# Loading W_v head by head, filler matmuls, an evenly spread conv finish and GLU blocks through a contiguous tile, in a hybrid conformer and attention block

## The chip, the cores and the metric

The kernel runs on the 8 cores of one Trainium2 chip, one batch element on each core (2048 positions of 2048 channels). The metric is the device time of the slowest core, in microseconds (us). Executions come in two states. In the slow one the cores of a die are recorded at a lower TensorE clock and the time is some per cent longer.

PE is TensorE, ACT is ScalarE, DVE is VectorE, POOL is GpSimd and SP is SyncE.

## The reference, cut to what matters

```python
h = rms_norm(x, ln1_g)
u = einsum("bsd,de->bse", h, w_in)                  # 2048 -> 5 x 1024
c_val, c_gate, q, k, v = split(u)
# conv_mixer(c_val, c_gate, ...)
g = c_val * sigmoid(c_gate)                         # GLU
y = causal_depthwise_conv(g, w_dw, width=31) + b_dw
y_conv = silu(layer_norm(y, over channels))
# attention in chunks of 64, each over itself and 8 chunks before, with a bias by distance
y_attn = chunked_relbias_attention(q, k, v, ...)
y = concat([rms_norm(y_conv), rms_norm(y_attn)])    # 1024 + 1024 channels
x = x + einsum("bse,ed->bsd", y, w_out)
x = x + relu(rms_norm(x) @ w_ff1)**2 @ w_ff2        # 2048 -> 8192 -> 2048
```

## The kernel before

The program is first recorded as a list of operations. A greedy list scheduler, which works with modelled durations, then puts them into one fixed order for each engine. The scheduler's rule is short (its latencies and its DMA rate are not measured here):

```python
# every engine: take, of the operations modelled as ready, the one that comes first in the program
o.prio = o.i + self.off
...
for s in succ[i]:                       # when a consumer becomes ready, in the model
    lat = XLAT                          # 180 ns from engine to engine
    if so.eng == "pe" and e != "pe":
        lat += SLACK                    # 400 ns more before PE may count on a result
    rt[s] = max(rt[s], o.end + lat)
...                                     # a DMA: bytes / DMA_BPNS (310) after the DMA before it, + 2000 ns
```

Stage 1 normalizes 16 tiles of x (128 rows each), transposes them on PE into `hT`, and multiplies them with W_v, which comes in four quarters of 256 columns:

```python
for j in range(4):
    ld.append(P.dma("pool", f"wv{j}", wv[:, j, :, :], wv_d[j]))
    ...                                          # x tiles 1 to 4 after quarter 0
for t in range(NT):
    norm_tile(xs1[t % 5], t, ...)                # squares on ACT, scaling on DVE, 16 PE transposes
    ...
    for hf in range(4):
        for k in range(16):
            mm(ps(hf, 0, 256), hT[:, qd, k, ti*128:(ti+1)*128], wv[:, hf, k, :], k == 0, k == 15)
        act(V[:, t, 2*hf:2*hf+2, 0:128], ..., AF.Identity)
```

Stage 2 is the q and k projection with the attention. Stage 3 is the conv: for each of 8 channel blocks (`cc`) and 4 row quarters (`qd`) two gate products, the GLU, and a depthwise product with Toeplitz matrices (`pad`). The GLU result `G` is transposed in 32x32 blocks by DVE straight into the scattered layout of `Gt`:

```python
stt(G[:, :], th[:, :], 1.0, ps(1), ALU.add, ALU.mult)
o_ = bass.AP(gt, 1 + 16 * qd, [[32 * 66, 128], [1, 16], [66, 32]])     # 66 elements from one to the next
P.vtr(o_, G[:, :].rearrange("p (b i) -> p b i", i=32), slow=3.6)
```

Stage 4 finishes the conv (LayerNorm, SiLU, sums of squares) while the output projection already runs. For a row quarter, `fin_cc` does this eight times:

```python
def fin_cc(qd, cc):
    stt(yy, yy, pc(bdw2 + cc), ysum[qd], ALU.add, ALU.subtract)   # DVE
    tt(yy, yy, rs[:, :], ALU.mult)                                 # DVE
    act(z, yy, AF.Silu, ...)                                       # ACT; in the trace y<-y,pv
    P.ts(yb[:, s, qd, 0, :], z, pc(goc + cc), ALU.mult)            # DVE
    act(jk, z, AF.Square)                                          # ACT; in the trace yb<-y, for quarter 0
    for j in range(4):
        mm(..., jk[j], onesb[:, 0:1], ...)                         # PE, 1 column: onesb,yb

def out_tr(t):                                                     # attention half of tile t
    for k in range(8): P.tr(...)                                   # PE: identb,on
    act(yT[:, :, :], ..., AF.Identity)                             # ACT: yT<-ps

def out_attn(t):
    ... mm(ps(b), yT[:, k, :], wo[:, 0, cb, k, :], ...)            # PE: wo,yT, 32 of 512 columns
...
for c in range(8):
    fin_cc(0, c)
fin_end(0)
...
out_tr(0)
out_attn(0)
```

After the last gate product, PE has only the depthwise rest, the small sums `onesb,yb` and the projection `wo,yT` to do. That hand-over from the gates to the projection is called **the switch** below. Stage 5 is the feed-forward part (FFN).

## Time and profile before

2785.49 us median (four fast runs, 2784.37 to 2788.06). From the profiled run's milestones, the mean of the 8 cores:

| part of the kernel | us |
|---|---|
| start to last W_v matmul | 181.6 |
| attention, to its last matmul before the gates | 320.8 |
| gates, to the last gate matmul | 226.0 |
| switch, from the last gate matmul to the last depthwise matmul | 34.7 |
| output projection, to the last `wo,yb` | 241.3 |
| FFN, from its first `hTb,yb` to the end | 1773.8 |
| end, with 1.9 between the last `wo,yb` and the FFN | 2780.1 |

A milestone is the start of the last matmul with the named operands, if not said otherwise.

The engine table and the shares of the chain of waits, on the profile page of the kernel before (busy us, share of the span, instructions; then the share of each engine in the chain that ended last):

```profile
PE 2707.2 (97%) x14445; PEld 1327.1 (48%) x14704; DVE 932.3 (34%) x1482; ACT 830.9 (30%) x1601; POOL 228.1 (8%) x365
...
PE 94%; DMA 2%; issue 2%; DVE 1%; ACT 1%; ACTq 0%; DVEq 0%; SPq 0%; POOLq 0%
```

PE is busy 97% of the time, and the chain is 94% PE. What can be won is PE's idle and half-clock time. By the view of stretches most of it lies at the start and, in smaller part, behind the switch (start:end, length, busy us and instructions of PE, of its weight loads, of DVE, ACT and POOL, then granted clock, DMA share, GB/s), kernel before, core 0:

```profile
20.00:60.00 40.00, 18.55 (x149) 14.06 (x147) 17.29 (x17) 19.30 (x31) 1.26 (x3) 0.74 1.00 261
700.00:900.00 200.00, 185.16 (x1246) 91.70 (x1268) 157.31 (x216) 121.36 (x167) 34.01 (x33) 0.97 0.55 144
```

From 20 to 60 us PE works less than half of the time, at a mean clock of 0.74, while the DMA engines are full (1.00). The waits of PE in the whole run say what it waits for (total us, times, longest), kernel before:

```profile
PE ps L163 <- DVE hb_78 L198: 10.7, 6, 4.4
PE ps L163 <- DVE hb_77 L198: 10.3, 5, 3.2
PE ps L163 <- DVE hb_79 L198: 7.1, 1, 7.1
```

`hb` is a normalized x tile. PE waits for tiles that arrive one by one, beside whole quarters of W_v: from issue to landing an x tile took 15.1 to 26.8 us (medians by buffer, core 0, 0 to 80 us) and a quarter 15.0 us. The groups of instructions show the cost of the scattered transpose (busy us and mean ns after the bar, idle time before), kernel before:

```profile
L206 DVE STREAM_TRANSPOSE Gt_112<-G 128x512 bf16<-128x512 bf16 x16 | 39.3, 2458 | 1.5
```

### The profile page before, as it was taken

What the parts mean: (1) busy time and instruction counts of PE and PEld (TensorE: products, weight loads), DVE (VectorE), ACT (ScalarE), POOL (GpSimd) and SP (SyncE); (2) the same over time, 40 slices, a digit from 0 to 9 for tenths busy, and PEclk for the clock granted to TensorE, in tenths of its full rate; (3) what the DMA queues carried; (4) which work ended last, traced back from release to release, by engine and by line L of the source; (5) the groups of instructions that cost most, each with busy time, mean ns of one, the idle gap of its engine ahead of it and who ended that gap; (6) DMA issues with size and microseconds to landing.
All of it is one profiled execution on the core that took longest, in us unless ns stands there. A gap on an engine that the chain in (4) does not pass through costs nothing.

```text
span 2782.1 us, 38484 instructions; the slowest of 8 cores (2778.2 to 2782.1 us)
## 1 busy us (share of the span) xinstructions
PE 2707.2 (97%) x14445; PEld 1327.1 (48%) x14704; DVE 932.3 (34%) x1482; ACT 830.9 (30%) x1601; POOL 228.1 (8%) x365
## 2 busy tenths in 40 slices
PE   4999999999989999999999999999999999999999
PEld 3875555444444544444444444444444444444444
DVE  3236665655787522022131130220311302202113
ACT  4428887311376431211202102112022021120120
POOL 0000000422500000000000000000000000000000
PEclk8999999999999999999999999999999999999999
DMA  9411110324655478454444444579544444444424
GB/s 243 103 31 36 34 28 11 61 46 76 122 152 167 152 155 177 77 76 76 76 76 76 76 76 76 76 151 196 123 76 76 76 76 76 76 78 76 77 43 137
DMA packets 112455, 256.86 MB, mean 92 GB/s; under 512 B 5393, under 2 KB 83217, under 8 KB 94609
## 3 DMA queue, kind: packets, MB, share of 16 engines
q0 software_dynamic: 92112, 167.82, 37.9%
q1 hardware_dynamic: 20162, 86.56, 9.3%
q8 instruction: 122, 2.00, 0.3%
q14 instruction: 59, 0.48, 0.1%
HBM read 388.60 MB, written 33.55 MB: 152 GB/s over the span
## 4 chain that ended last, share of the span: by engine, by line
PE 94%; DMA 2%; issue 2%; DVE 1%; ACT 1%; ACTq 0%; DVEq 0%; SPq 0%; POOLq 0%
PE ps L159 93%; DMA xa_71<-x 1%; PE ps L163 1%; DMA acc<-out 1%; DMA wc_105<-wcg 0%; DVE y L198 0%; DVE y L192 0%; DVE hb_77 L198 0%; DVE Gt_113 L206 0%; ACT L178 0%; ACT hb_77 L178 0%; DVE hb_78 L198 0%; DVE y L206 0%; DVE yb L203 0%; DVE h2b L198 0%
## 5 line engine op out<-in xcount | busy, mean ns | idle before, releaser
L192 DVE TENSOR_TENSOR acc<-acc,ps 128x512 f32<-128x512 f32 x512 | 351.8, 688 | 1413.3 <-PE ps L159 1401.9
L159 PE MATMUL ps<-yb,fT 128*128 128x512 bf16 x2699 | 596.4, 379 | 4.0 <-DVE acc L192 1.1
L159 PEld LDWEIGHTS ps<-yb,fT 128*128 128x128 bf16 x2752 | 269.1, 98 | 326.3 <-issue 2.1
L178 ACT ACTIVATE rl_134<-ps 128x512 f32<-128x512 f32 x128 | 76.4, 597 | 1102.5 <-PE ps L159 1101.0
L159 PE MATMUL ps<-w2s_138,fT 128*128 128x512 bf16 x1317 | 292.4, 379 | 1.4
L159 PE MATMUL ps<-hTb,yb 128*128 128x512 bf16 x1024 | 242.2, 379 | 0.0
L159 PE MATMUL ps<-yb 128*128 128x512 bf16 x992 | 237.6, 379 | 1.7
L159 PEld LDWEIGHTS ps<-w2s_138,fT 128*128 128x128 bf16 x1344 | 131.5, 98 | 158.6
L225 POOL DMA_DIRECT2D yb<-w x75 | 66.6, 888 | 1173.8 <-PE ps L159 1105.6
L159 PEld LDWEIGHTS ps<-yb 128*128 128x128 bf16 x1024 | 100.2, 98 | 120.8
L159 PEld LDWEIGHTS ps<-hTb,yb 128*128 128x128 bf16 x1024 | 100.2, 98 | 120.3
L178 ACT ACTIVATE rl_135<-ps 128x512 f32<-128x512 f32 x128 | 76.4, 597 | 271.1 <-PE ps L159 271.1
L159 PE MATMUL ps<-wv,hT 128*128 128x256 bf16 x1024 | 120.6, 281 | 5.4 <-DMA wv<-wv 4.0
L159 PE MATMUL ps<-hTb,w1s_136 128*128 128x512 bf16 x512 | 121.0, 379 | 0.0
L159 PE MATMUL ps<-hTb,w1s_137 128*128 128x512 bf16 x512 | 121.0, 379 | 0.0
L159 PE MATMUL ps<-wo,yT 128*128 128x512 bf16 x497 | 117.1, 383 | 3.9 <-ACT yT L178 2.2
L159 PE MATMUL ps<-yb,w1s_136 128*128 128x512 bf16 x480 | 119.3, 379 | 1.7
L159 PE MATMUL ps<-yb,w1s_137 128*128 128x512 bf16 x496 | 117.5, 379 | 0.8
L159 PE MATMUL ps<-hT,wc_105 128*128 128x512 bf16 x498 | 115.0, 381 | 3.4 <-DMA wc_105<-wcg 2.5
L159 PE MATMUL ps<-hT,wc_104 128*128 128x512 bf16 x496 | 117.4, 379 | 0.9
L159 PE MATMUL ps<-wo,yb 128*128 128x512 bf16 x496 | 113.4, 379 | 0.8
L159 PEld LDWEIGHTS ps<-wv,hT 128*128 128x128 bf16 x1024 | 102.6, 101 | 20.6 <-issue 6.3
(300 smaller groups left out, 2741.1 us busy)
## 6 DMA issues: line engine op xcount, KB each, us to landing
yb<-w POOLq DMA_DIRECT2D x75, 1024.0 KB, 10.2
w2s_138<-w POOLq DMA_DIRECT2D x21, 1024.0 KB, 9.5
w1s_136<-w POOLq DMA_DIRECT2D x16, 1024.0 KB, 9.3
w1s_137<-w POOLq DMA_DIRECT2D x16, 1024.0 KB, 9.4
acc<-out SPq DMA_DIRECT2D x16, 1024.0 KB, 11.8
out<-acc SPq DMA_DIRECT2D x64, 256.0 KB, 7.5
wo<-wo POOLq DMA_DIRECT2D x8, 1024.0 KB, 13.4
xs_127<-x SPq DMA_DIRECT2D x6, 1024.0 KB, 6.4
```

Of the source, the lines that this page charges most:

```text
L159: self.op("pe", lambda e: e.matmul(out, lhsT=lhsT, rhs=rhs, start=start, stop=stop, skip_group_check=skip), [lhsT, rhs], [out], f * max(n ...
L163: self.op("pe", lambda e: e.transpose(out, in_, ident), [in_, ident], [out], 64.0)
L178: self.op("act", lambda e: e.activation(out=out, in_=in_, func=func, scale=scale, bias=bias, **kw), r, w, d).func = func
L192: self._ew(eng, lambda e: e.tensor_tensor(out=out, in0=in0, in1=in1, op=op), [in0, in1], [out], fast)
L225: o = self.op(eng, lambda e: e.dma_start(out=out, in_=in_), r, w, 900.0 if eng == "pool" else 350.0, dma=True, key=key, nbytes=nb)
```

## The change

The intent: (1) load x tiles and single heads of W_v in turn, two loads in flight, so that PE has work early; (2) fill PE's early gaps with matmuls of ones, meant to keep its clock from being halved (before, core 0's was recorded at 0.50 from 36.7 to 53.8 us); (3) transpose the GLU blocks into a contiguous tile, and let ACT do the reordering copy; (4) spread the conv finish evenly over the output tiles, and let the scheduler count on results for PE 300 ns later (SLACK). The core of the diff:

```diff
-SLACK = 400.0
+SLACK = 700.0
-DMA_BPNS = 310.0
+DMA_BPNS = 320.0
...
+    def fill_gaps(self, until, reach):     # after scheduling: matmuls of ones where the model sees PE idle
...
         self.schedule()
+        self.fill_gaps(60000.0, 0.8)
...
+LAZY = 0.0                                 # optional extra slack for some matmuls, unused at 0
...
-    wv_d = dr("wv", [4, 128, 16, 256])
+    wv_d = dr("wv", [8, 128, 16, 128])
...
+    chain = [o_gr, xo_[0]]
+    for it in ("w0", "x1", "w1", "x2", "w2", "x3", "w3", "x4", "w4", "x5", "w5", "x6", "w6", "x7", "w7"):
...
+        chain.append(o_)
...
-        for hf in range(4):
-            for k in range(16):
-                mm(ps(hf, 0, 256), hT[:, qd, k, ti * 128:(ti + 1) * 128], wv[:, hf, k, :], k == 0, k == 15)
-            act(V[:, t, 2 * hf:2 * hf + 2, 0:128], ..., AF.Identity)
+        for e0, n in VG[min(t, 8)]:        # heads that are there already, in groups of 4, 2 or 1
+            vgroup(t, e0, n)
+        if t < 8:
+            for tt_ in range(t + 1):       # the new head for all tiles so far
+                vgroup(tt_, t, 1)
+    for k in range(2, len(chain)):
+        chain[k].deps.add(chain[k - 2].i)  # two loads in flight
...
+    Gc = sb("Gc", [512], BF16, D0 + 34 * KB)      # shares its place with th and yT
...
-        o_ = bass.AP(gt, 1 + 16 * qd, [[32 * 66, 128], [1, 16], [66, 32]])
-        P.vtr(o_, G[:, :].rearrange("p (b i) -> p b i", i=32), slow=3.6)
+        P.vtr(Gc[:, :], G[:, :])
+        act(gt[:, :, 1 + 16 * qd:17 + 16 * qd], bass.AP(Gc, 0, [[512, 128], [1, 32], [32, 16]]), AF.Identity)
...
-    seq = [("c", 0), ("f", 1, 0, 4), ("a", 2), ("c", 1), ("f", 1, 4, 8), ("c", 2), ("s", 2), ("a", 3), ("c", 3), ("f", 2, 0, 3), ...
+    seq = [("c", 0), ("f", 1, 0, 2), ("a", 2), ("c", 1), ("f", 1, 2, 5), ("c", 2), ("f", 1, 5, 8), ("a", 3), ("c", 3), ("s", 2), ...
```

In `seq`, "a" and "c" are the two halves of an output tile, "s" the statistics and "f" pieces of the finish of a row quarter.

More of the change, by code (lines that the diff above doesn't have):

```diff
@@ L22 @@
 XLAT = 180.0
-SLACK = 400.0
+SLACK = 700.0
 TABLE = 1300.0
 DMA_LAT = 2000.0
-DMA_BPNS = 310.0
+DMA_BPNS = 320.0
 SEM_EPOCH = 30000
+FILL = 216.0
 class Op:
-    __slots__ = ("i", "func", "eng", "fn", "dur", "deps", "dma", "key", "cnt", "bytes", "prio",
+    __slots__ = ("i", "func", "lazy", "eng", "fn", "dur", "deps", "dma", "key", "cnt", "bytes", "prio",
                  "start", "end", "pos", "signal", "waits", "ins")
@@ L47, in __init__ @@
         self.func = None
+        self.lazy = 0.0
 class Prog:
@@ L154, in n, with mm @@
         return k
-    def mm(self, out, lhsT, rhs, start, stop, skip=False):
+    def mm(self, out, lhsT, rhs, start, stop, skip=False, lazy=0.0):
         n = self.n(rhs)
@@ L159, in mm, with filler @@
         self.op("pe", lambda e: e.matmul(out, lhsT=lhsT, rhs=rhs, start=start, stop=stop, skip_group_check=skip),
-                [lhsT, rhs], [out], f * max(n / 2.37, 64.0))
+                [lhsT, rhs], [out], f * max(n / 2.37, 64.0)).lazy = lazy
+    def filler(self, out, lhsT, rhs):
+        self.fill = (lambda e: e.matmul(out, lhsT=lhsT, rhs=rhs, start=True, stop=True, skip_group_check=True),
+                     [self.last_w[k] for k in self.keys(lhsT)][0])
+    def fill_gaps(self, until, reach):
+        fn, dep = self.fill
+        order, t = [], 700.0
+        for o in self.order["pe"]:
+            k = max(0, int((o.start - t - SLACK - XLAT) * reach / FILL)) if o.start < until else 0
+            for _ in range(k):
+                f = Op(len(self.ops), "pe", fn, FILL)
+                f.deps.add(dep)
+                f.start = f.end = o.start
+                self.ops.append(f)
+                order.append(f)
+                self.seq.insert(self.seq.index(o), f)
+            order.append(o)
+            t = max(t, o.end)
+        for j, o in enumerate(order):
+            o.pos = j
+        self.order["pe"] = order
     def tr(self, out, in_, ident):
@@ L296, in schedule @@
                 if so.eng == "pe" and e != "pe":
-                    lat += SLACK
+                    lat += SLACK + so.lazy
                 rt[s] = max(rt[s], o.end + lat)
@@ L482, in build_program @@
     wqk = [sb(f"wqk{i}", [16, 128], BF16, o + 16384 + 4096 * i) for i in range(3)]
-    wv = sb("wv", [4, 16, 256], BF16, C)
+    wv = sb("wv", [8, 16, 128], BF16, C)
     on = sb("on", [16, 1024], BF16, C)
@@ L493, in loadx @@
         xo_[t] = P.dma("sp", f"xa{t % 5}", xs1[t % 5][:, :], x_d[t * 128:(t + 1) * 128, :])
+        return xo_[t]
     def bcast(g, n):
         return bass.AP(gv_d.tensor, g * 2048, [[0, 128], [1, n]])
+    P.memset(onesb[:, :], 1.0, "dve")
+    P.memset(onef[:, :], 1.0, "dve")
+    P.filler(ps(3), onesb[:, :], bass.AP(onesb, 0, [[128, 128], [0, 4], [1, 128]]))
     gr = sb("gr", [2048], F32, D0 + 42 * KB)
-    P.dma("sp", "gr", gr[0:1, :], gv_d[0:1, :])
+    o_gr = P.dma("sp", "gr", gr[0:1, :], gv_d[0:1, :])
     loadx(0)
@@ L502, in build_program @@
     P.dma("sp", "pv", pv[:, :], pv_d)
-    P.memset(onef[:, :], 1.0, "dve")
     for j in range(4):
@@ L509, in build_program @@
             act(g1[:, j * 512:(j + 1) * 512], ps(4 + j), AF.Identity)
-    ld = []
-    for j in range(4):
-        ld.append(P.dma("pool", f"wv{j}", wv[:, j, :, :], wv_d[j]))
-        if j == 0:
-            for t in range(1, 5):
-                loadx(t)
-            P.dma("sp", "sel", sel[:, :], id_d[:, 0:4])
+    chain = [o_gr, xo_[0]]
+    for it in ("w0", "x1", "w1", "x2", "w2", "x3", "w3", "x4", "w4", "x5", "w5", "x6", "w6", "x7", "w7"):
+        j = int(it[1])
+        if it[0] == "w":
+            o_ = P.dma("pool", f"wv{j}", wv[:, j, :, :], wv_d[j])
+        elif j < 5:
+            o_ = loadx(j)
+        else:
+            o_ = ("x", j)
+        chain.append(o_)
+    P.dma("sp", "sel", sel[:, :], id_d[:, 0:4], after=chain[4].i)
     P.ts(pv[:, bdw2:bdw2 + 8], pv[:, bdw:bdw + 8], 2.0, ALU.mult)
@@ L519, in build_program @@
     tt(pc(gqk), pc(52), pc(53), ALU.mult)
-    P.memset(onesb[:, :], 1.0, "dve")
     P.memset(oh[:, :], 0.0, "dve")
@@ L539, in norm_tile, with vgroup @@
             dst(hf, psh[:, b * 1024:(b + 1) * 1024].rearrange("p (k c) -> p k c", c=128))
+    VG = []
+    for t in range(9):
+        e, gs = 0, []
+        while e < t:
+            n = next(n for n in (4, 2, 1) if e % n == 0 and e + n <= t)
+            gs.append((e, n))
+            e += n
+        VG.append(gs)
+    nvb = [0]
+    def vgroup(t, e0, n):
+        qd, ti = divmod(t, 4)
+        b = nvb[0] % 3
+        nvb[0] += 1
+        for k in range(16):
+            rhs = wv[:, e0:e0 + n, k, :] if n > 1 else wv[:, e0, k, :]
+            mm(ps(b, 0, 128 * n), hT[:, qd, k, ti * 128:(ti + 1) * 128], rhs, k == 0, k == 15)
+        act(V[:, t, e0:e0 + n, 0:128], ps(b, 0, 128 * n).rearrange("p (h c) -> p h c", c=128), AF.Identity)
     for t in range(NT):
@@ L555, in build_program @@
             mark = len(P.ops) - 1
-        for hf in range(4):
-            for k in range(16):
-                mm(ps(hf, 0, 256), hT[:, qd, k, ti * 128:(ti + 1) * 128], wv[:, hf, k, :], k == 0, k == 15)
-            act(V[:, t, 2 * hf:2 * hf + 2, 0:128], ps(hf, 0, 256).rearrange("p (h c) -> p h c", c=128), AF.Identity)
-    for j in (1, 2, 3):
-        ld[j].deps.add(xo_[2 * j - 1].i)
+        for e0, n in VG[min(t, 8)]:
[3 more added lines that the diff above has]
+                vgroup(tt_, t, 1)
+    chain = [xo_[c[1]] if isinstance(c, tuple) else c for c in chain]
+    for k in range(2, len(chain)):
+        chain[k].deps.add(chain[k - 2].i)
+    for t in range(8, NT):
+        xo_[t].deps.add(chain[-2].i)
     q32 = [sb(f"q32{i}", [512], F32, D0 + 40 * KB + 2048 * i) for i in range(2)]
@@ L592, in proj @@
                     for j in range(4):
-                        mm(ps(2, j, j + 1), sq[b][:, j * 128:(j + 1) * 128], onesb[:, 0:1], True, True)
+                        mm(ps(2, j, j + 1), sq[b][:, j * 128:(j + 1) * 128], onesb[:, 0:1], True, True, lazy=LAZY)
                     act(kst[:, qd, :], ps(2, 0, 4), AF.Ln, scale=1.0 / 128, bias=pc(epsc))
@@ L717, in conv_dw @@
             act(cs[:, :], yy, AF.Square, scale=0.5, bias=pc(bdw + cc))
-            mm(ps(7)[0:4, :], oh[:, 3 - qd:7 - qd], cs[:, :], cc == 0 and qd == 0, cc == 7, skip=True)
+            mm(ps(7)[0:4, :], oh[:, 3 - qd:7 - qd], cs[:, :], cc == 0 and qd == 0, cc == 7, skip=True, lazy=LAZY)
             su = ysum[qd][:, :]
@@ L760, in fin_cc @@
         for j in range(4):
-            mm(ps(FB, j, j + 1), bass.AP(jk.tensor, jk.offset + j * 128, [list(jk.ap[0]), [1, 128]]), onesb[:, 0:1], cc == 0 and j == 0, cc == 7, skip=True)
+            mm(ps(FB, j, j + 1), bass.AP(jk.tensor, jk.offset + j * 128, [list(jk.ap[0]), [1, 128]]), onesb[:, 0:1], cc == 0 and j == 0, cc == 7, skip=True, lazy=LAZY)
     def fin_end(qd):
@@ L859, in build_program @@
     fin_stats(1)
-    seq = [("c", 0), ("f", 1, 0, 4), ("a", 2), ("c", 1), ("f", 1, 4, 8), ("c", 2), ("s", 2), ("a", 3), ("c", 3), ("f", 2, 0, 3),
-           ("a", 4), ("c", 4), ("f", 2, 3, 6), ("a", 5), ("c", 5), ("f", 2, 6, 8), ("a", 6), ("c", 6), ("s", 3), ("a", 7), ("c", 7),
-           ("f", 3, 0, 3), ("a", 8), ("c", 8), ("f", 3, 3, 6), ("a", 9), ("c", 9), ("f", 3, 6, 8)]
-    for t in range(10, NT):
+    seq = [("c", 0), ("f", 1, 0, 2), ("a", 2), ("c", 1), ("f", 1, 2, 5), ("c", 2), ("f", 1, 5, 8), ("a", 3), ("c", 3), ("s", 2),
+           ("a", 4), ("c", 4), ("f", 2, 0, 2), ("a", 5), ("c", 5), ("f", 2, 2, 5), ("a", 6), ("c", 6), ("f", 2, 5, 8), ("a", 7), ("c", 7), ("s", 3),
+           ("a", 8), ("c", 8), ("f", 3, 0, 3), ("a", 9), ("c", 9), ("f", 3, 3, 6), ("a", 10), ("c", 10), ("f", 3, 6, 8), ("a", 11), ("c", 11)]
+    for t in range(12, NT):
         seq += [("a", t), ("c", t)]
@@ L984, in _prep_shared @@
     wvv = win[:, 4096:5120]
-    wv = np.stack([kc(wvv[:, i * 256:(i + 1) * 256], 256) for i in range(4)])
+    wv = np.stack([kc(wvv[:, i * 128:(i + 1) * 128], 128) for i in range(8)])
     wcg = np.stack([np.stack([kc(win[:, o + i * 128:o + (i + 1) * 128], 128) for o in (0, 1024)], 1) for i in range(8)])
```

## The prediction

> **What bounds the kernel now.** TensorE: the engine table gives PE 2707 of 2782 us busy (97%), the chain of waits is 94% PE. Only time in which PE is idle or half-clocked can be won. By the table of stretches it is lost in two places.
>
> (a) Start, 0 to 75.5 us. PE is dense only from 75.5 us (timeline). By then it has done 8 tiles' transposes (128 at 56 ns) and 114 of the 1024 W_v matmuls (256 columns, 109 ns apart when dense): about 20 us of useful work. The DMA share is about 1.0 from 2 to 67 us: 12 x tiles and the 4 W_v quarters move in 65 us. [...] With whole quarters PE has little to do per loaded byte; the waits list charges 28 us to hb (tiles arriving late). Short bursts also leave the granted clock at 0.50 from 37 to 53 us and near 62 and 72 us. [...]
>
> (b) Conv finish, 700 to 900 us: PE idle 12.4 + 2.4 us, three half-clock steps nearby; waits on ACT yb, jk, yT, cs, rct; DVE is 83 to 100% busy at 730-750 us. 500-700 us loses about 5 more. The FFN (PE over 99%) doesn't change.
>
> **What the change does.**
> 1. x0,w0,...x7,w7, at most two in flight. After pair t, 2t+1 units (tile x head, 16 x 56 ns = 0.9 us) become ready, against about 6.6-7 us per pair of loads: PE becomes dense near tile 3 to 4, at 38-45 us, with 18-20 us of work done. The last pair lands at 55-62 us. 640 narrow matmuls at 56 ns, 64 at 109, 320 at 215 come to the same 112 us, so narrow groups cost nothing. W_v now ends at 182 us; I expect 147 to 160: gain 28 us (22 to 36), all on the critical path. The static order assumes DMA times; where they are late PE stalls, so I don't book the full 36.
> 2. Some 35 fillers of 0.22 us (0.43 cold), nearly all before tile 0 is transposed. They cost at most 1-2 us and keep the clock up: 2-4 us, counted in 1.
> 3. GLU blocks: 32 DVE transposes of 2.46 us with scattered output become contiguous ones (estimate 0.4-0.75 us, from 0.73 us for the f32 transpose of y) plus an ACT copy (estimate 0.6-0.75 us, from 0.62 us for jk). DVE sheds about 55 us, ACT gains about 20; off the path except near 730-750 us.
> 4. Even finish and larger slack: the stalls at 730-750 and 790-805 us shrink. 3 and 4 together: 9 us (2 to 16) of about 24.
>
> **Predicted: 2785.6 - 28 - 9 = 2749 us**, 80% range 2736 to 2764. Faster by over 2% (under 2730): 0.05; within 2%: 0.94; slower: 0.01.
>
> **What would show it.** W_v's last matmul at 147-160 us; PE dense from 40-45 us, no long 0.50 clock after 15 us; DVE transposes of G under 0.8 us; PE idle at 700-900 us halved; the FFN's length unchanged to 2 us.
>
> **What would make it wrong.** Gaps between loads with two in flight: DMA share well below 1 before 60 us, PE dense only after 55 us, gain 15 us. The new order or ACT's extra copies stalling PE in the conv stage (step 4 gives nothing). Conversely, if start and finish both reach their floor, 2730.

The "6.6-7 us per pair of loads" are the author's estimate; at the 259 GB/s recorded from 2 to 67 us a pair (1536 KB) would take 6.1 us. What the trace of before shows are half-clock records that last 3.41 us or a multiple of it, but for each core's last one: on core 0 17.07 us of them from 36.7 us on, with PE busy for 5.26 us from 37 to 53 us. That fillers would keep the clock up, and for 2 to 4 us, was the author's estimate.

## The result, and the profile after

The changed kernel has fast runs of 2768.62 and 2766.56 us. Two more were slow (2981.03 and 2956.98) and are not used. The ratio is 0.9934, with a 95% interval of 0.9911 to 0.9958: 0.66% faster, in the class "within 2%". A ratio here is the mean time of one kernel's fast runs over that of the other's fast runs of the same rounds, so it is not quite the ratio of the quoted medians. The predicted 2749 us, range 2736 to 2764, is missed: the two runs lie 2.6 and 4.6 us above the range, and about half of the gain came.

Milestones, the mean of 8 cores of the profiled runs (both fast):

| part | before | after | change | predicted |
|---|---|---|---|---|
| start to last W_v matmul | 181.6 | 161.1 | -20.5 | -28 |
| attention | 320.8 | 318.5 | -2.3 | 0 |
| gates | 226.0 | 227.1 | +1.1 | -9 for gates, switch and output together |
| switch | 34.7 | 41.7 | +7.0 | |
| output projection | 241.3 | 237.1 | -4.2 | |
| FFN | 1773.8 | 1774.2 | +0.4 | 0 |
| end | 2780.1 | 2761.6 | -18.5 | -37 |

So two things are to be explained: 7.5 us that are missing at the start, and a conv stage that lost 3.9 us where 9 were to be won. The switch is the worst line of the table.

The page of the kernel after, in the same two views as shown of before:

```profile
PE 2729.5 (99%) x14737; PEld 1299.8 (47%) x14737; DVE 880.7 (32%) x1482; ACT 871.2 (31%) x1641; POOL 229.0 (8%) x369
...
PE 94%; DMA 4%; ACT 1%; issue 1%; DVE 1%; SPq 0%; ACTq 0%; DVEq 0%; POOLq 0%
```

PE's 99% looks better than it is: half-clocked matmuls and fillers count as busy too (the first 27 fillers for 10.4 us, on core 0 at 427 ns each until 17.2 us and not 216). DMA has doubled its share of the chain. The stretches of the kernel after, core 0, with the two worst of 10 us added:

```profile
20.00:60.00 40.00, 33.78 (x423) 28.09 (x424) 18.59 (x19) 22.45 (x47) 2.64 (x5) 0.91 0.92 210
700.00:900.00 200.00, 183.48 (x1171) 89.85 (x1171) 148.38 (x210) 136.96 (x179) 16.92 (x16) 0.92 0.49 140
710.00:720.00 10.00, 2.15 (x52) 1.82 (x52) 9.91 (x14) 8.65 (x15) 5.72 (x6) 0.51 1.00 204
720.00:730.00 10.00, 8.01 (x36) 3.40 (x37) 5.43 (x7) 5.10 (x9) 1.71 (x2) 0.64 0.35 67
```

PE's idle time at 700 to 900 us was 14.8 us and is 16.5 us now, where I predicted half. From 710 to 720 us PE is busy for only 2.15 us, and the clock stays near half afterwards (its records on core 0 say half from 710.2 us on, for 17.1 us). The start has improved a lot, but the DMA share fell from 1.00 to 0.92. The groups of the GLU transpose after:

```profile
L231 DVE STREAM_TRANSPOSE Gc<-G 128x512 bf16<-128x512 bf16 x32 | 22.7, 710 | 2.9
L203 ACT ACTIVATE Gt_113<-Gc 128x512 bf16<-128x512 bf16 x16 | 17.1, 1072 | 43.0 <-DVE Gc L231 42.9
```

The transpose fell from 2458 to 710 ns, as predicted. The ACT copy takes 1072 ns, where I had estimated 600 to 750. Its output lies in runs of 16 elements but its input is read with a stride of 32. A contiguous ACT operation of that size from f32 (`yb<-y`) takes 614 ns here; no run tests the stride alone. In the whole program DVE lost 51.6 us of work and ACT gained 40.3, twice the 20 predicted; 34.2 of these are the copies. In the scattered output of the old DVE transpose neighbours lay 66 elements apart; the traces show that it is slower (2458 ns against 710), not why.

### Where the start loses

The chain of waits of the kernel after begins like this (start, length, what):

```profile
1.48 5.01 DMA xa_71<-x
6.56 8.51 DMA xa_72<-x
15.14 6.87 DMA xa_73<-x
...
69.64 3.73 PE ps L161 x64
```

Each x tile is issued only when the x tile before it has landed (each load waits for the one two before it in an alternating list). On core 0 a pair of loads takes 7.43 us: the heads of W_v were issued at 12.64 and, six pairs later, at 57.22 us. Core 0 has the slowest pairs; the mean of the 8 cores is 7.20 us. I had predicted 6.6 to 7 us for a pair, and PE dense from 38 to 45 us. PE is dense only from 69.6 us. The last head of W_v had landed at 64.8 us, so the loads alone don't explain this. The timeline of ACT, core 0, shows what stood in between:

```profile
67.33 1.91 ACT L203 ACTIVATE hb_79<-xa_74 128x2048 bf16<-128x2048 f32 x1 [2.18 <-DMA xa_74<-x]
69.23 0.59 ACT L203 ACTIVATE V<-ps 128x128 bf16<-128x128 f32 x3
```

ACT idles for 2.18 us until the ninth x tile lands, and the copy of `V` that PE needs stands behind the work on this tile. So PE's waits up to 165 us name a second suspect, ACT (kernel after, core 0; the mean of the cores is 9.7 us for both lines together):

```profile
PE ps L161 <- ACT V L203: 4.2, 2, 2.3
PE ps L161 <- ACT hT L203: 2.6, 2, 2.2
```

### Where the switch loses

PE's timeline after the last gate matmul, kernel after, core 0 (start, length, operands, count, and in brackets the idle time before and what ended it):

```profile
711.84 0.25 PE L161 MATMUL ps<-onesb,yb 128*128 128x1 bf16 x4 [4.06 <-ACT yb L203]
715.14 0.24 PE L161 MATMUL ps<-onesb,yb 128*128 128x1 bf16 x4 [3.06 <-ACT yb L203]
...
722.48 1.44 PE L161 MATMUL ps<-wo,yT 128*128 128x512 bf16 x3 [1.48 <-ACT yT L203]
```

For 15 us PE does little but tiny sums, each waiting for ACT. The projection `wo,yT`, which would fill the time, begins at 722.48 us. It needs `yT`, and the timeline of ACT shows where that copy stands, first before and then after:

```profile
732.53 1.02 ACT L178 ACTIVATE yT<-ps 128x1024 bf16<-128x1024 bf16 x1 [1.09 <-PE ps L159]
...
734.87 0.81 ACT L178 ACTIVATE y<-y,pv 128x512 f32<-128x512 f32 x1
```

```profile
709.38 0.81 ACT L203 ACTIVATE y<-y,pv 128x512 f32<-128x512 f32 x1
710.10 1.08 ACT L203 ACTIVATE Gt_114<-Gc 128x512 bf16<-128x512 bf16 x1
711.08 0.61 ACT L203 ACTIVATE yb<-y 128x512 bf16<-128x512 f32 x1
...
720.51 0.80 ACT L203 ACTIVATE y<-y,pv 128x512 f32<-128x512 f32 x1
721.22 1.00 ACT L203 ACTIVATE yT<-ps 128x1024 bf16<-128x1024 bf16 x1
```

Before, the copy of `yT` came ahead of the first SiLU (`y<-y,pv`). After, all eight SiLU operations stand ahead of it, with seven of their squares, though the transposes it needs were done by 707 us. ACT works through its list in that order: the copy starts only at 721.22 us, 14 us after those transposes.

### The profile page after: what moved, and what is told of

Same layout as the page of the kernel before. It is cut to its first block, busy times and chain, and to the rows that moved or that the text cites. A ratio compares the mean times of both kernels' runs of the same rounds, so it can differ in the third digit from the quotient of the medians.

```text
span 2767.1 us, 38913 instructions; the slowest of 8 cores (2756.5 to 2767.1 us)
## 1 busy us (share of the span) xinstructions
PE 2729.5 (99%) x14737; PEld 1299.8 (47%) x14737; DVE 880.7 (32%) x1482; ACT 871.2 (31%) x1641; POOL 229.0 (8%) x369
## 4 chain that ended last, share of the span: by engine, by line
PE 94%; DMA 4%; ACT 1%; issue 1%; DVE 1%; SPq 0%; ACTq 0%; DVEq 0%; POOLq 0%
PE ps L161 93%; DMA acc<-out 1%; PE ps L188 1%; DMA xa_74<-x 1%; DMA xa_72<-x 1%; DMA xa_73<-x 1%; DMA xa_71<-x 0%; DMA wc_105<-wcg 0%; ACT L203 0%; DVE y L217 0%; DVE yb L228 0%; DVE hb_77 L223 0%; DVE acc L217 0%; DVE y L223 0%; ACT h2b L203 0%
## 5 line engine op out<-in xcount | busy, mean ns | idle before, releaser
L161 PE MATMUL ps<-wv,hT 128*128 128x128 bf16 (+2 forms) x1024 | 117.9, 277 | 7.7 <-ACT V L203 4.2
L161 PE MATMUL ps<-wo,yT 128*128 128x512 bf16 x512 | 123.6, 395 | 1.7 <-ACT yT L203 1.7
L161 PEld LDWEIGHTS ps<-wv,hT 128*128 128x128 bf16 x1024 | 75.0, 99 | 48.6 <-issue 11.5
```

The source lines that it names most:

```text
L161: self.op("pe", lambda e: e.matmul(out, lhsT=lhsT, rhs=rhs, start=start, stop=stop, skip_group_check=skip), [lhsT, rhs], [out], f * max(n ...
```

## The experiments

Theories.

- Start. **A**: two loads in flight are too few, since each x tile waits for the landing of the one before. **B** (rival): the static order on ACT, made with a DMA model that doesn't fit, puts the work for a late x tile ahead of the copies `V` and `hT` that PE needs. **C** (rival): the fillers matter, for better or worse.
- Switch. **D**: the cheaper GLU makes the finish of quarter 0 ready earlier, so the greedy scheduler, which takes the lowest program index first, puts it on ACT ahead of `yT` (whose place is also only free after the last `Gc` copy). **E** (rival): the larger SLACK did it. **F** (rival): the new `seq` did it. **G** (rival): the extra ACT work itself did it, whatever the order.

All twelve experiments gave correct results. "Fast runs" are those used; slow ones are left out.

| kernel | W_v end | attention | gates | switch | output | FFN | mean end | timed dies | fast runs |
|---|---|---|---|---|---|---|---|---|---|
| before | 181.6 | 320.8 | 226.0 | 34.7 | 241.3 | 1773.8 | 2780.1 | 2780.5 | 2784.37 to 2788.06 |
| after | 161.1 | 318.5 | 227.1 | 41.7 | 237.1 | 1774.2 | 2761.6 | 2760.8 | 2768.62, 2766.56 |
| e_glu_old | 161.3 | 320.3 | 225.3 | 39.0 | 236.3 | 1773.6 | 2757.8 | 2757.3 | 2762.53 to 2769.14 |
| e_yt_first | 161.0 | 318.5 | 227.7 | 33.7 | 236.5 | 1773.3 | 2752.7 | 2753.7 | 2758.50 to 2768.49 |
| e_slack400 | 159.8 | 319.1 | 227.8 | 42.1 | 232.3 | 1774.5 | 2757.6 | 2756.6 | 2768.37 |
| e_seq_old | 160.2 | 318.5 | 227.4 | 41.9 | 242.2 | 1773.4 | 2765.7 | 2766.2 | 2773.17, 2773.42 |
| e_nofill | 160.0 | 318.5 | 226.7 | 41.6 | 238.8 | 1774.3 | 2761.8 | 2763.7 | 2767.76, 2775.28 |
| e_chain4 | 156.0 | 318.5 | 228.0 | 41.5 | 235.5 | 1774.9 | 2756.4 | 2756.8 | 2761.94 |
| e_bpns280 | 156.6 | 319.1 | 227.3 | 42.0 | 236.3 | 1773.3 | 2756.6 | 2756.5 | 2760.13, 2762.91 |
| e_yt_slack400 | 159.4 | 319.0 | 228.1 | 33.4 | 232.6 | 1773.6 | 2748.0 | 2748.4 | 2754.25, 2758.61 |
| e_before_glu | 181.8 | 319.5 | 227.2 | 42.5 | 241.8 | 1773.7 | 2788.3 | 2788.1 | 2795.61 |
| e_glu_old_s400 | 160.3 | 320.3 | 225.7 | 33.8 | 232.5 | 1773.9 | 2748.6 | 2748.6 | 2755.91 |
| e_best1 | 155.7 | 319.7 | 226.8 | 33.4 | 236.9 | 1773.6 | 2748.1 | 2748.6 | 2752.22 to 2755.15 |
| e_best1_lazy (cores 4 to 7) | 155.9 | 319.4 | 227.4 | 30.8 | 233.7 | 1773.6 | 2742.8 | 2742.2 | 2744.67 to 2746.44 |

Segments are means of the profiled run's cores. The profiled run of the last kernel fell in the slow state, so only its undisturbed die is used. For the same four cores the mean end is 2779.9 before, 2760.4 after and 2748.6 in e_best1. The last column is the device time of the slowest core, which lies a few us above its span in a profile (before: 2783.66 in the profiled run, against 2782.1). Several rows rest on one fast run. As a check, "timed dies" is the mean end over every die, in all runs of a kernel, whose cores were all granted at least 0.985 of the clock. The dies of one kernel scatter by 0.3 to 2.8 us (standard deviation), so differences of 2 us or less show nothing. Edits are against the changed kernel unless said otherwise.

### The GLU change taken back (e_glu_old)

```diff
-        P.vtr(Gc[:, :], G[:, :])
-        act(gt[:, :, 1 + 16 * qd:17 + 16 * qd], bass.AP(Gc, 0, [[512, 128], [1, 32], [32, 16]]), AF.Identity)
+        o_ = bass.AP(gt, 1 + 16 * qd, [[32 * 66, 128], [1, 16], [66, 32]])
+        P.vtr(o_, G[:, :].rearrange("p (b i) -> p b i", i=32), slow=3.6)
```

> The changed kernel with the GLU blocks put back to the scattered DVE transpose, nothing else. The stretch from the last gate matmul to the last depthwise matmul (mean of 8 cores) is 34.7 us before and 41.7 us changed. Theory (the cheaper GLU makes the first SiLU ready earlier, so the list scheduler puts the copy of yT on ScalarE behind seven SiLUs, and PE, which needs yT, stands still): the stretch returns to about 35 us, and the span falls by 5 to 8 us against the changed kernel. Rival (the larger slack or the even finish is what reordered it): the stretch stays at 41 to 42 us and the span rises or stays.

The switch is 39.0, against 41.7 after and 34.7 before, and the mean end 2757.8, 3.8 better than after. The ratio is 0.9929 (0.9910 to 0.9949). Taking the GLU change back helps, which favours D or G, but it closes only part of the gap: I had expected about 35. Something else also upsets the switch when the GLU is old.

### The copy of yT first (e_yt_first)

```diff
+    P.off = -2000      # rank these nine operations 2000 places earlier
     out_tr(0)
+    P.off = 0
```

> The changed kernel with one thing added: the transposes of tile 0 of the attention output and their copy to yT get a higher priority in the scheduler. Theory (order of ScalarE is the cause, the work itself is not): the stretch from the last gate to the last depthwise matmul falls from 41.7 us to 28 to 34 us, the half-clock window near 710 us shrinks or goes, span 8 to 13 us shorter than the changed kernel. Rival (VectorE and ScalarE are simply too busy there, with 32 more ScalarE copies of 1.08 us): PE waits somewhere else instead, stretch stays above 39 us.

This leaves every operation as it is and changes only the order. The switch falls from 41.7 to 33.7 and the mean end by 8.9 us to 2752.7. The ratio is 0.9921 (0.9896 to 0.9946). The timed dies give 7.1 us (2760.8 to 2753.7). The work on ACT is the same, so G falls: it is the order, as D says. One part of D stays untested by itself, the shared place: here too `yT` is copied only after the last `Gc` copy (714.96 and 713.47 us on core 0). PE's timeline, core 3 of this kernel:

```profile
714.43 0.25 PE L161 MATMUL ps<-onesb,yb 128*128 128x1 bf16 x4 [4.51 <-ACT yb L203]
715.45 4.42 PE L161 MATMUL ps<-wo,yT 128*128 128x512 bf16 x10 [0.77 <-ACT yT L203]
```

The projection starts right after the first sum. One wait of 4.5 us is left, since that first sum still stands ahead of `wo,yT` in PE's own list.

### SLACK back to 400 (e_slack400)

```diff
-SLACK = 700.0
+SLACK = 400.0
```

> The changed kernel with the scheduler's slack back to 400 ns. Theory (slack has no part in the stall at 706-722 us): last gate to last depthwise matmul stays at 41 to 42 us. If slack caused it: about 35 us. The attention stretch (last W_v matmul to last PV matmul), 320.8 us before and 318.5 us changed, returns to 320 or more if the slack gave those 2.3 us. W_v may end 0 to 4 us later than 161.1.

The switch is 42.1, so E alone falls. The output projection, however, takes 232.3 against 237.1: the larger slack costs 4.8 us there. Two more pairs of kernels that differ in the slack alone give 3.9 and 3.8 (e_yt_first and e_yt_slack400, e_glu_old and e_glu_old_s400). Only one run was fast, so this kernel has no ratio; the segments come from a fast profiled run.

### The old sequence of the finish (e_seq_old)

```diff
-    seq = [("c", 0), ("f", 1, 0, 2), ("a", 2), ("c", 1), ("f", 1, 2, 5), ...
+    seq = [("c", 0), ("f", 1, 0, 4), ("a", 2), ("c", 1), ("f", 1, 4, 8), ...
```

> The changed kernel with the old, uneven order of the conv finish. Theory: the stall near 706-722 us comes from the GLU change, so last gate to last depthwise matmul stays at 41 to 42 us; and the even order is what shortened the next stretch (last depthwise to last output matmul) from 241.3 to 237.1 us, so this returns to 240 to 242 us and the span grows by 3 to 5 us. Rival (the cheaper GLU relieves VectorE there): the stretch stays at 237 us.

The switch is unchanged (41.9) and the output takes 242.2 against 237.1. F falls. The even finish is worth 5.1 us, the one part of step 4 that does what it was meant to do. The ratio is 0.9961 (0.9932 to 0.9990).

### No fillers (e_nofill)

```diff
-        self.fill_gaps(60000.0, 0.8)
```

> The changed kernel without its 33 filler matmuls, order of all else as it was. In the changed kernel W_v ends at 161.1 us (mean of 8 cores). Theory (the serial chain of x loads, 1.5 to 67 us, sets the start; the fillers only fill): W_v ends within 1.5 us of 161.1, with more half-clock time before 60 us, and tile 0 is transposed 2 to 4 us earlier than 18.7 us. Rival (the fillers matter by keeping the clock up): W_v ends 3 to 6 us later. Third possibility (they delay tile 0 and with it the rest): W_v ends 2 to 4 us earlier.

W_v ends at 160.0 against 161.1, the mean end is 2761.8 against 2761.6, and the ratio is 0.9950 (0.9929 to 0.9972), with two fast runs that lie 7.5 us apart. At the start the 33 fillers win nothing that can be measured. The timed dies leave up to 3 us open (2763.7 against 2760.8), which is not clear of the scatter.

In the first 100 us the recorded half-clock time, the mean of cores, is 25.6 us before, 6.4 after and 5.7 without fillers: with the new loading order it is small with or without fillers. PE's work is denser there (31.93 us busy from 20 to 60 us without fillers, against 18.55 before, core 0). These figures leave out the time before a core's first clock record, in which matmuls run at half speed (on core 0, see below, 427 ns for 512 columns against 216). The first record of full clock comes at 27.6 us before, 11.1 after and 20.9 without fillers. So with the fillers full clock is recorded earlier, but little work is there to use it. The first lines of PE's timeline, after and then without fillers (both core 0):

```profile
1.48 4.00 PE L166 MATMUL ps<-onesb 128*128 128x512 bf16 x9 [1.48 <-DVE oh L240]
5.41 7.19 PE L161 MATMUL ps<-gr,onef 1*128 1x512 f32 x8
12.53 6.37 PE L166 MATMUL ps<-onesb 128*128 128x512 bf16 x18
18.74 1.06 PE L188 MATMUL ps<-identb,hb_77 128*128 128x128 bf16 x16
```

```profile
2.90 7.16 PE L161 MATMUL ps<-gr,onef 1*128 1x512 f32 x8 [2.90 <-DMA gr<-gvec]
12.92 2.10 PE L188 MATMUL ps<-identb,hb 128*128 128x128 bf16 x16 [2.86 <-DVE hb L223]
```

On core 0 the fillers run at 427 ns each (4.00 over 9, a little over, since the last one's length is in it), twice the 216 ns that they take later, and this pitch lasts until 17.2 us. They hold up the first 16 transposes by 6 us and then save them 1 us. The first record of full clock comes there only after some 15.7 us of back-to-back matmuls, but among them are four one-row f32 products (8 records), and on other cores of the same run it comes sooner. Core 3, two lines of PE's timeline and one stretch (its clock is the third figure from the end):

```profile
5.41 3.81 PE L161 MATMUL ps<-gr,onef 1*128 1x512 f32 x8
9.15 5.69 PE L166 MATMUL ps<-onesb 128*128 128x512 bf16 x18
9.20:12.40 3.20, 3.20 (x9) 1.11 (x9) 1.47 (x5) 2.66 (x5) 0.00 (x0) 0.50 1.00 197
```

Its clock record says full at 5.67 us, 4.2 us after the first filler, and the f32 products take 3.81 us instead of 7.19. At 9.08 us, with these products running all the while, the record falls back to half. At 12.49, after 3.3 us of further fillers, it is full again. In the eleven kernels with fillers 54 of the 88 cores do this: full at 4.1 to 6.2 us, half again 3.41 us later. On the other 34 the first record of full clock comes at 16.5 to 17.7 us, during the second group of fillers (core 0: from 12.53 us on). So on the 54 cores full clock was recorded 2.6 to 4.7 us after the first filler. The one-row f32 products did not bring it in 7.19 us on core 0, and on core 3 it fell back while they ran. Why the cores differ is not shown.

### Four loads in flight (e_chain4)

```diff
-    for k in range(2, len(chain)):
-        chain[k].deps.add(chain[k - 2].i)
+    for k in range(4, len(chain)):
+        chain[k].deps.add(chain[k - 4].i)
```

> The changed kernel with four loads in flight in place of two (each waits for the load four before it), nothing else. Theory (with two in flight each queue restarts its load only after the last one has landed, so the DMA share is 0.88 to 0.96 between 20 and 60 us and a pair of loads takes 7.4 us, not 6.6): share about 1.0, a pair about 6.7 us, the last W_v head lands 4 to 6 us earlier, W_v ends at 155 to 158 us. Rival (memory bandwidth is the limit, packets just take longer): the pair stays at 7.2 us or more and W_v ends within 1.5 us of 161.1.

A pair of loads takes 6.29 us instead of 7.59 (core 0; the last six heads, issued from 16.52 to 47.99 us here and from 19.27 to 57.22 after; the mean of cores is 6.27 against 7.30). W_v ends at 156.0, 5.1 us earlier. Theory A holds. PE's waits for ACT's `V` and `hT` fell as well, from 9.7 to 3.8 us (mean of cores). The stretch, core 0 of this kernel:

```profile
20.00:60.00 40.00, 35.95 (x442) 29.92 (x443) 18.98 (x19) 24.74 (x50) 2.64 (x5) 0.91 0.99 252
```

The DMA share is 0.99 again, where the kernel after had 0.92, and the rate is 252 GB/s, where it had 210. The quickest loads in the kernel after, 128 KB each by SP's queue, took a median of 2.0 to 2.3 us to landing, and two loads in flight leave 8% of the DMA time unused where four leave 1%. What fills this gap is not shown. This kernel had one fast timed run, so its 2761.94 us has no interval.

### Another DMA rate in the scheduler's model (e_bpns280)

```diff
-DMA_BPNS = 320.0
+DMA_BPNS = 280.0
```

> The changed kernel with the scheduler told a slower DMA (280 in place of 320 bytes/ns), so that PE and ScalarE orders fit the measured arrivals. Theory (late arrivals, not order, set the start): W_v ends within 1.5 us of 161.1. Rival (ScalarE stands before late x tiles while copies of V and hT that PE needs wait behind it): the waits of PE for ACT V and hT (6.8 us on core 0) fall below 3 us and W_v ends 2 to 5 us earlier.

Not a byte moves otherwise, only the static order differs. W_v ends at 156.6, 4.5 us earlier, and the ratio is 0.9914 (0.9893 to 0.9936). Theory B holds as well. PE's waits up to 165 us, this kernel, core 0:

```profile
PE ps L161 <- ACT V L203: 1.9, 3, 1.1
PE ps L161 <- ACT hT L203: 0.8, 2, 0.4
```

On core 0, which the lines of the kernel after are from too, the two fall from 6.8 to 2.7 us, and in the mean of the cores from 9.7 to 4.5. A pair of loads still takes 7.13 us (7.20 after, means of cores). So both A and B are right, each worth about 5 us, but e_best1 shows below that they don't add. The waits say why: either cure takes away the same waits of PE for ACT, one by loads that land in time for the static order, the other by an order that fits the late loads.

### yT first and SLACK 400 together (e_yt_slack400)

```diff
-SLACK = 700.0
+SLACK = 400.0
...
+    P.off = -2000
     out_tr(0)
+    P.off = 0
```

> Candidate: the changed kernel with the priority of yT raised and the slack at 400. If the two effects measured apart add up: mean end of the cores 2761.6 - 8.9 - 4.0 = 2748.7 us, last depthwise matmul near 741 us, the stretch from there to the last output matmul near 232 us. If the slack acted only by moving the same stall: 2752 to 2754 us.

Switch 33.4 and output 232.6: the two effects add, and the mean end is 2748.0. Gates, switch and output together take 294.1 us, against 302.0 before and 305.9 after. That is 7.9 us less than before, close to the 9 which the prediction had booked for steps 3 and 4.

### The GLU change alone, in the kernel before (e_before_glu)

The edit is made to the kernel before:

```diff
+    Gc = sb("Gc", [512], BF16, D0 + 34 * KB)
...
-        P.vtr(o_, G[:, :].rearrange("p (b i) -> p b i", i=32), slow=3.6)
+        P.vtr(Gc[:, :], G[:, :])
+        act(gt[:, :, 1 + 16 * qd:17 + 16 * qd], bass.AP(Gc, 0, [[512, 128], [1, 32], [32, 16]]), AF.Identity)
```

> The kernel before with the GLU change alone (contiguous transpose and ScalarE copy). If the GLU change alone flips the order on ScalarE: W_v still ends at 181.6 us; last gate to last depthwise matmul rises from 34.7 us to 41 to 43 us; the attention stretch falls by about 2 us (320.8 to 319), the gate stretch rises by 1 to 2 us (226.0 to 227.5); the span is 5 to 8 us LONGER than before. Rival (the loss needs the larger slack or the new loads too): stretch near 35 us, span as before or a little shorter.

The switch is 42.5 against 34.7, and the mean end 2788.3 against 2780.1. The GLU change alone, with 50.0 us less work for DVE (932.3 to 882.3), makes the kernel **8.2 us slower**. Only one timed run was fast, but the undisturbed die of the slow one says the same (2787.7). PE's waits from 640 to 830 us, first before, then before with the GLU change alone, then after:

```profile
PE ps L159 <- ACT yb L178: 2.4, 3, 1.3
```

```profile
PE ps L159 <- ACT yb L178: 13.0, 7, 4.1
```

```profile
PE ps L161 <- ACT yb L203: 10.5, 6, 4.1
```

The same wait of 4.1 us, from the same cause, appears with no part of the change but this one. Attention is 1.3 us shorter here than before, so at least a part of the attention's unexpected 2.3 us seems to come with it; 320.3 with the old GLU in e_glu_old says the same. I have not followed how.

### Old GLU and SLACK 400 (e_glu_old_s400)

```diff
-SLACK = 700.0
+SLACK = 400.0
...
-        P.vtr(Gc[:, :], G[:, :])
-        act(gt[:, :, 1 + 16 * qd:17 + 16 * qd], ..., AF.Identity)
+        P.vtr(o_, G[:, :].rearrange("p (b i) -> p b i", i=32), slow=3.6)
```

> The changed kernel with the scattered transpose and slack 400, which closes the square (new GLU 700: 41.7; new GLU 400: 42.1; old GLU 700: 39.0 us from last gate to last depthwise matmul). If either of the two is enough to upset the order (the order of PE puts 13 matmuls with yT ahead of the first sum here): 34 to 36 us, and the output stretch near 232 us. If the 4.3 us that the old GLU alone did not give back have another cause: 38 to 40 us again.

Switch 33.8, output 232.5, mean end 2748.6. This closes the square, with the means of cores:

| | SLACK 700 | SLACK 400 |
|---|---|---|
| new GLU | 2761.6 (switch 41.7) | 2757.6 (42.1) |
| old GLU | 2757.8 (39.0) | 2748.6 (33.8) |
| new GLU, yT first | 2752.7 (33.7) | 2748.0 (33.4) |

With the order of `yT` set right, the new GLU (2748.0) and the old (2748.6) are equal. Sparing DVE some 50 us of work is worth nothing that can be seen here, since DVE isn't what PE waits for. Within the scatter, the whole effect of the GLU change was the order that it caused. The old GLU with `yT` first was not run. With the old GLU the larger slack also spoils the switch, by 5.2 us, which is why e_glu_old recovered only a part.

### All corrections (e_best1), and the sums last (e_best1_lazy)

e_best1 puts `yT` first, with SLACK 400, four loads in flight and DMA_BPNS 280:

```diff
-SLACK = 700.0
+SLACK = 400.0
-DMA_BPNS = 320.0
+DMA_BPNS = 280.0
...
-    for k in range(2, len(chain)):
-        chain[k].deps.add(chain[k - 2].i)
+    for k in range(4, len(chain)):
+        chain[k].deps.add(chain[k - 4].i)
...
+    P.off = -2000
     out_tr(0)
+    P.off = 0
```

e_best1_lazy adds to that:

```diff
-LAZY = 0.0
+LAZY = 1500.0      # the one-column sums may wait: other matmuls go ahead of them
```

> Candidate: changed kernel with yT first, slack 400, four loads in flight and the slower DMA figure of 280. Mean end of the cores 2748.0 us with the first two; four loads in flight gave 5.1 and the DMA figure 4.5 us at the start. If both attack the same idle time: W_v ends at 154 to 156 us, mean end 2743 to 2745. If they add: W_v ends at 150 to 152 us, mean end near 2739.

> The candidate with the change's own unused knob set: LAZY 1500 ns, so that PE's order puts the small column sums behind 23 matmuls with yT in place of before them. PE still waits 4.5 us for the first of these sums (yb) with yT first. If that wait is order alone: last gate to last depthwise matmul falls from 33.4 us to 27 to 30 us, no half-clock window near 710 us, mean end 3 to 6 us less than the candidate. Rival: the wait turns up at the next user of yT or of VectorE, less than 1.5 us gained.

e_best1: fast runs 2752.22 to 2755.15, ratio 0.9890 (0.9873 to 0.9907). W_v ends at 155.7, hardly earlier than with either correction of the start alone. PE's waits for ACT's `V` and `hT` are down to 0.3 us (mean of cores). What is left are 3.9 us of waiting for W_v's own loads, with the DMA engines full (share 1.03 from 20 to 40 us and 0.98 from 40 to 60, core 0). So the loads themselves seem to be the next limit; no run tests it. The output takes 236.9 rather than 232.6, though its slack is 400. This is a miss, also of the expected end (2748.1, not 2743 to 2745), and I have not followed it up. PE idles for 4.5 us in this stretch, as with the larger slack (4.6 after), where e_yt_slack400 idles for 2.0 (means of cores).

e_best1_lazy: fast runs 2744.67, 2745.70 and 2746.44, ratio 0.9863 (0.9846 to 0.9879). It beats both kernels, and by mean end it is 5.8 us better than e_best1 on the same four cores. PE's timeline at the switch, core 6:

```profile
705.81 6.45 PE L161 MATMUL ps<-wo,yT 128*128 128x512 bf16 x22 [3.46 <-ACT yT L203]
712.10 0.24 PE L161 MATMUL ps<-onesb,yb 128*128 128x1 bf16 x4
```

Now 22 matmuls of the projection stand ahead of the first sum, which no longer makes PE wait. The switch is 30.8, shorter than before the change, though not the 27 to 30 expected. A wait of 3.5 us for `yT` itself remains.

## Why the prediction was right or wrong

- **Right: the bound and the class.** PE bounds the kernel and only its idle and half-clock time can be won; the FFN stayed (1773.8 and 1774.2); the change is within 2%.
- **Step 1, right in mechanism, too large in size.** I booked 28 us (22 to 36), and it measured 20.5. W_v ends at 161.1, just outside 147 to 160. The step that failed is "PE becomes dense near tile 3 to 4, at 38-45 us": on core 0 this came at 69.6 us. Two terms were mis-sized. The pair of loads, "about 6.6-7 us", took 7.20 (mean of cores), since each x tile waits for the landing of the one before, and the last head landed at 63.2 us (mean) rather than 55 to 62. I had named this danger (gaps between loads with two in flight), and its signs came: share 0.92, PE dense only after 55 us. And I had booked no figure for the stalls that I did mention, of a static order that assumes other DMA times: PE waited 9.7 us for ACT's `V` and `hT`. e_chain4 and e_bpns280 win 5.1 and 4.5 us there, and both shorten these waits.
- **Narrow groups cost nothing: right.** Pitches of 56, 109 and 216 ns (medians) were recorded for 128, 256 and 512 columns.
- **Step 2, wrong.** The fillers were to keep the clock up, worth 2 to 4 us at the start. With them full clock is first recorded some 10 us earlier (11.1 against 20.9), but W_v ends no earlier for it (161.1 with them, 160.0 without).
- **Step 3, right in DVE's cost, wrong in ACT's.** DVE's transpose went to 710 ns (under 0.8 us, as predicted), and the ACT copy to 1072 ns rather than 600 to 750.
- **Steps 3 and 4 together, wrong in sign.** "3 and 4 together: 9 us" became a loss of 3.9 us over gates, switch and output. The failed step is "off the path except near 730-750 us": I took the GLU change for a shift of work from one engine that is not critical to another, and left out that it re-sorts ACT's list. In its place all eight SiLUs stood ahead of the copy of `yT` on ACT, and PE stood still for it. Shown by e_before_glu (+8.2 us alone) and e_yt_first (-8.9 us by order alone; -7.1 by the timed dies). Of the rest, the even order gave 5.1 us, as hoped, and the larger SLACK took 4.8 us back (e_seq_old, e_slack400). "The new order ... stalling PE in the conv stage" stood in the prediction's own list of dangers, without a probability to match.
- **Attention -2.3 us, not predicted.** About half of it or more comes with the GLU change; how is open.

Added up from kernels that differ in nothing else: with old GLU and SLACK 400 the rest of the change is worth 31.5 us (2780.1 to 2748.6), of the 37 predicted. The GLU change and the slack together turn this into 18.5.

Open: why e_best1's output is slower than e_yt_slack400's; whether the loads alone stop the start at 156 us; and what triggers the slow state. What it looks like, the one slow profile (e_best1_lazy) shows: not half the clock, but 0.81 of it. Cores 0 and 1 were recorded at 0.81 for 602 us from 29 us on, cores 2 and 3 for 573 us from 2268 us on, the other die never. A stretch of core 0 (clock third from the end):

```profile
100.00:600.00 500.00, 495.26 (x2652) 242.66 (x2695) 223.88 (x561) 280.28 (x724) 42.25 (x139) 0.81 0.15 27
```

Matmuls of 512 columns came every 263 ns there, against 216. In the slowest of the timed runs the slow die has a mean clock of 0.81 to 0.82, which fits 0.81 throughout; these runs have no profile.

## What to carry to other kernels

In a statically ordered program, a cheaper operation is also a change of the order: before booking a gain for relieving an engine, compare the instruction lists around each place where the bottleneck engine is handed new work, and give what feeds it priority explicitly. Cost a chain of loads by its issue times (with two in flight, each waited for a landing), and allow enough loads in flight that the DMA share stays at 1 (here two took 7.59 us a pair at a share of 0.92, four 6.29 us at 0.99; core 0). Ask what stands behind a late load in each engine's list. Undo each part of a change singly and compare segments over all cores: here an even order (5.1 us won), a larger slack (4.8 us lost) and a cheaper transpose (some 8 us lost when made alone) hid behind one small total.
